# The last quarter of a second MLP product, from four plain tiles to seven quarter products

## The chip, the cores and the metric

One core of a Trainium2 chip runs the whole program in one launch. The metric is the time of an execution in microseconds on the device. The kernel is written by hand in a tile language: the program names tiles and instructions, and a scheduler at compile time orders each engine's instructions (earlier program text first, among those it believes ready), assigns buffers and inserts the waits. Where the text asks for it, an engine's order is fixed as written.

## The reference

Two layers of a hybrid decoder block on 512 tokens of width 1024, all in float32. Each layer has a mixing part (a gated delta rule and a sliding-window attention, both fed by one input projection, merged and projected by `w_o`), and then an MLP:

```python
h2 = rmsnorm(x, pre_mlp_g)
ff = jnp.square(jax.nn.relu(h2 @ w_ff1)) @ w_ff2      # 1024 -> 4096 -> 1024
return x + rmsnorm(ff, post_mlp_g)
```

The change is in `@ w_ff2` and in what follows it: the norm of `ff`, the residual, and the norm with which the next layer begins.

## The kernel before

**Products in three parts.** TensorE multiplies pairs of rounded values. Every float32 operand is split into a high part (a cast on ScalarE) and a low part (the value less its high part, on VectorE), and a product is the sum of high x high, high x low and low x high: three matmuls. `split` (L406, L407) does so for activations, `prefetch` (L319 the cast `wh`, L320 the difference `wl`) for weights.

**Weights in chunks.** All weights are packed in the order in which they are used, as chunks of 128 x 1024 numbers (512 KB; 128 x 864 in the first part of the input projection). `load` (L269) fetches one by a DMA on SyncE's queue (SP) into one of five buffers `wr`; `weights()` hands out the next split chunk and has `prefetch` run four ahead (`LOOK`), each into one of four `wh` and `wl` buffers.

**The MLP in quarters.** `w_ff1` has 4096 columns, taken in four quarters `s` of 1024. In each, `mm_a` forms eight blocks of 128 hidden units x 512 tokens in PSUM (24 matmuls each), ScalarE applies relu and the square, and the quarter's 1024 rows of `w_ff2` are multiplied in. The sum over the quarters is in `acc[t][n]`: four tiles `t` of 128 tokens, two halves `n` of 512 columns.

**Quarters 0 to 2: seven products.** The quarter's product, 512 tokens x 1024 hidden units x 1024 columns, is cut in two in every direction, and a Strassen-Winograd scheme forms it from seven half-size products P1 to P7 in place of eight. `lefts` makes the left factors (sums and differences of halves of the hidden values, then seven splits, on VectorE and ScalarE) for each half of the hidden block. `seven` makes the right factors as a running sum of weight blocks (`add`, L285, on VectorE), in 14 chunks. `mm_c` (L395, L397, L399) does one product: two chunks x two token tiles x two k-blocks x three = 24 matmuls of 512 columns; with `onto` it adds to a PSUM tile that holds an earlier product. The order is P1, P5, P6, P4, P7, P2, P3. Results are drained to `acc` by VectorE or ScalarE (`into`, L1232 and L1234; L1289, L1301, L1309), and six adds of SBUF tiles go to POOL (`ptt`, L1293 and L1303). Tokens 0 and 1 are complete only after P2 and P3, tokens 2 and 3 after P7.

**Quarter 3: plain.** Eight blocks of hidden values are split to `h3`; `mm_b4` multiplies them by the left 512 columns of `w_ff2` for all four tiles, chunk by chunk (L382 to L384), and VectorE adds the result to `acc[t][0]`, ScalarE sums its squares (`meansq`, L426) and VectorE multiplies by the gain (L1328). The right 512 columns follow tile by tile (`mm_b`, L355 to L357), and each finished tile is passed to `ff2_tail`.

**The tail of a tile.** `ff2_tail` calls `post_tile`: load the residual (`xt`, two DMAs, L468, into buffers T[5] and T[6] that quarters 0 to 2 use for the left factors of P1 and P2), add the last product (L471), sum of squares, `rstd` (a sum L433 and a power on POOL, L434), the gain (L474), scale and add the residual (L475, L476). In layer 1 the tile is then written out (L1240). In layer 0 it is stored to `xd` (L1242), `norm_scale` applies the next norm (another two sums of squares, a power on POOL, `xs` on VectorE, L446), and `norm_turn` transposes it (TensorE, L455) and splits it (L459, L461) into the left side of the next layer's projection.

**The order at the boundary.** In layer 0, `last_tiles` does tiles 0 and 1, then tiles 2 and 3 together, with the turns of tiles 0 and 1 put between their k-blocks. The next layer's first projection begins with tiles 0 and 1; the turns of tiles 2 and 3 are put between the halves of tile 1 there. TensorE's order over this whole stretch is fixed as written (`Order`). At the end of layer 1 nothing is fixed: four times `mm_b` and `ff2_tail`.

Of the kernel before, what the change touches and what calls it, by code (L numbers as in the profile page):

```python
# [20 lines left out]
P = 128  # L21
# [31 lines left out]
def chunk_order(depth):  # L53


    out = []
    for l in range(depth):
        a_in = lambda w, c: out.append(("chunk", w, l, 0, c, 0))
        b_in = lambda w, r, c, n: out.append(("chunk", w, l, r, c, n))
        for n in range(3):  # L60
            for j in range(4):
                b_in("w_in", j * 256, OFF_B + n * NB, NB)
        n_ = {"K": 0, "G": 0, "A": 0}
        for c in "".join(MIX):
# [12 lines left out]
        for m in range(KT):  # L77
            a_in("w_up_dn", m * P)
        for n in range(2):
            for j in range(4):  # L80
                b_in("w_o", j * 256, n * 512, 512)
        for s in range(4):
            for m in FF_ORDER if s < 3 else range(8):
                a_in("w_ff1", (s * 8 + m) * P)
            if s < 3:
                out.append(("seven", "w_ff2", l, s * 1024))
                continue
            for n in range(2):
                for j in range(4):
                    b_in("w_ff2", s * 1024 + j * 256, n * 512, 512)  # L90
    return out


# [26 lines left out]
def hybrid_trunk(ctx, tc, x, positions, pre_mix_g, dn_conv_w, dn_a_log, dn_dt_bias, dn_norm_g,  # L120
# [47 lines left out]
    def PM(name):  # L168
        return pm.tile([P, 512], F32, name=name, tag="pm")
# [105 lines left out]
    def seven(w, l, r0):  # L275


        held = {}

        def part(i, k, j):  # L280
            return load((w, l, r0 + i * 512 + j * 256, k * 512, 512))

        def add(j, o):
            a = held["a", j]
            tt(out=a, in0=a, in1=o, op=ALU.add)  # L285
# [13 lines left out]
        return [(lambda f=f, j=j: f(j), 512) for f in makes for j in range(2)]  # L299


    specs = []
    for kind_, *key in chunk_order(depth):
        if kind_ == "seven":
            specs.extend(seven(*key))
        else:
            specs.append((tuple(key), key[4]))
    pre = []
# [15 lines left out]
    def weights():  # L324
        i = used[0]
        used[0] += 1
        prefetch(i + LOOK)
        r, pre[i] = pre[i], None
        return r

    def mm_a(ps, aT, ks=range(KT), w=None):
        wh, wl = w = w or weights()
        for k in ks:
            hi, lo = aT[k]
            mm(ps, lhsT=wh[:, k, :], rhs=hi, start=k == 0, stop=False)  # L335
            mm(ps, lhsT=wh[:, k, :], rhs=lo, start=False, stop=False)  # L336
            mm(ps, lhsT=wl[:, k, :], rhs=hi, start=False, stop=k == KT - 1)  # L337
        return w
# [44 lines left out]
                    mm(pss[t], lhsT=hi[:, tsl], rhs=wl[:, r, :], start=False, stop=False)  # L383
                    mm(pss[t], lhsT=lo[:, tsl], rhs=wh[:, r, :], start=False, stop=k == KT - 1)  # L384

    def mm_c(pss, left, onto=False):

        for j in range(2):
            wh, wl = weights()
            hi, lo = left[j]  # L390
            for t in range(2):
                for r in range(2):
                    c = slice(r * 256 + t * P, r * 256 + (t + 1) * P)
                    first, last = j + r == 0 and not onto, j + r == 2
                    mm(pss[t], lhsT=hi[:, c], rhs=wh[:, r, :], start=first, stop=False,  # L395
                       skip_group_check=onto)
                    mm(pss[t], lhsT=hi[:, c], rhs=wl[:, r, :], start=False, stop=False,  # L397
                       skip_group_check=onto)
                    mm(pss[t], lhsT=lo[:, c], rhs=wh[:, r, :], start=False, stop=last,  # L399
                       skip_group_check=onto)  # L400

    def four(i):
        return [b("ps_b4") for b in ((PZ, PZ, PS, PS) if i % 2 else (PM, PM, PK, PS))]
# [5 lines left out]
    def pair(U, name):  # L409
        return U(name + "_h", F32R), U(name + "_l", F32R)  # L410
# [82 lines left out]
    for l in range(depth):  # L493
# [764 lines left out]
                split(src, *p_)  # L1258
                left[name].append(p_)

        for s in range(3):
            left = {f"P{i}": [] for i in range(1, 8)}
            raw = [None, None]
            for i, m in enumerate(FF_ORDER):
                if s == 0 and i < 4:
                    ps = early[i][0]
                else:
                    ps = PM("ps_f1")
                    mm_a(ps, h2)
# [24 lines left out]
            pc = [PM("ps_p4"), PM("ps_p4")]  # L1294
            mm_c(pc, left["P4"])
            for t in range(2):
                into(2 + t, 0, pc[t])
            pc = [PS("ps_p7"), PK("ps_p7")]
            mm_c(pc, left["P7"])
            for t in range(2):  # L1300
                tt(out=v_[t], in0=pc[t], in1=v_[t], op=ALU.add)  # L1301
                for n, op in ((0, ALU.subtract), (1, ALU.add)):
                    ptt(out=acc[2 + t][n], in0=acc[2 + t][n], in1=v_[t], op=op)  # L1303
            mm_c(pa, left["P2"], True)
            for t in range(2):
                into(t, 0, pa[t])
            mm_c(pb_, left["P3"], True)
            for t in range(2):
                tt(out=acc[t][1], in0=pb_[t], in1=acc[t][1], op=ALU.add)  # L1309


        gb3 = gain(post_mlp_g[l])
        h3 = []
        for m in range(8):
            ps = PM("ps_f1")
            mm_a(ps, h2)
            r_ = T[4]("relu")
            act(out=r_, in_=ps, func=AF.Relu)
            act(out=r_, in_=r_, func=AF.Square)
            p_ = pair(T[m % 4], "h3")  # L1320
            split(r_, *p_)
            h3.append(p_)
        pss = four(1)
        mm_b4(pss, h3)
        for t in range(NT):
            tt(out=acc[t][0], in0=pss[t], in1=acc[t][0], op=ALU.add)
            s0[t] = meansq(acc[t][0], "pq0", True)
            tt(out=acc[t][0], in0=acc[t][0], in1=gb3[:, :512], op=ALU.mult)  # L1328
        ws = [weights() for _ in range(4)]
        if l < depth - 1:  # L1330
            nxt = pre_begin(l + 1)
            xs_next = []
            order = Order(nc.tensor)
            order.begin()
            last_tiles(ws, h3, "ps_f2", ff2_tail, lambda t: norm_turn(xs_next[t], t, nxt[1]))
            hT = nxt
        else:
# [28 lines left out]
```

## Time and profile before

| | us |
|---|---|
| median of 3 runs | 1878.39 (1876.84 to 1881.92) |
| the profiled execution's own time | 1877.79 |
| its span, first to last instruction | 1876.1 |
| TensorE busy | 1847.1 (98%) |
| VectorE busy | 1278.7 (68%) |
| ScalarE busy | 937.7 (50%) |
| POOL busy | 279.9 (15%) |

The span is what the profile shows between the first and the last instruction; the execution's own time has 1.7 us more around it. The profile names the engines PE (TensorE; PEld is its loading of the left operand), DVE (VectorE), ACT (ScalarE), POOL (GpSimd) and SP (SyncE, here the queue of DMAs). L with a number is a line of the kernel; a line of a helper stands for all its callers. A row of a group gives busy time and mean duration, and then the time the engine stood idle before these instructions and what ended it. The granted clock of TensorE was 0.999 of full.

### The profile page before, as it was taken

What the parts mean: (1) busy time and instruction counts of PE and PEld (TensorE: products, weight loads), DVE (VectorE), ACT (ScalarE), POOL (GpSimd) and SP (SyncE); (2) the same over time, 40 slices, a digit from 0 to 9 for tenths busy, and PEclk for the clock granted to TensorE, in tenths of its full rate; (3) what the DMA queues carried; (4) which work ended last, traced back from release to release, by engine and by line L of the source; (5) the groups of instructions that cost most, each with busy time, mean ns of one, the idle gap of its engine ahead of it and who ended that gap; (6) DMA issues with size and microseconds to landing.
All of it is one profiled execution on the core that took longest, in us unless ns stands there. A gap on an engine that the chain in (4) does not pass through costs nothing. (4 is left out here: it accounts for less than half of the span.)

```text
span 1876.1 us, 26833 instructions
## 1 busy us (share of the span) xinstructions
PE 1847.1 (98%) x9716; PEld 1533.0 (82%) x9716; DVE 1278.7 (68%) x2434; ACT 937.7 (50%) x1909; POOL 279.9 (15%) x421
## 2 busy tenths in 40 slices
PE   8999999999999999999999999999999999999998
PEld 7888788888888888888888887888887888888886
DVE  5499795777656667684556997857775567586834
ACT  6677732344434645454456887233343346454442
POOL 1322102121100020211012231022111000111200
PEclk9999999999999999999999999999999999999999
DMA  5633436333363253554245333553334533534631
GB/s 179 201 117 114 122 124 193 103 123 103 90 213 129 87 191 101 169 168 169 84 143 187 103 128 102 161 171 104 122 96 116 190 121 103 178 124 153 196 122 45
DMA packets 123445, 255.40 MB, mean 136 GB/s; under 512 B 32609, under 2 KB 49313, under 8 KB 123314
## 3 DMA queue, kind: packets, MB, share of 16 engines
q1 hardware_dynamic: 123314, 253.71, 42.2%
q8 instruction: 76, 1.25, 0.3%
q14 instruction: 55, 0.45, 0.1%
HBM read 224.70 MB, written 28.97 MB: 135 GB/s over the span
## 5 line engine op out<-in xcount | busy, mean ns | idle before, releaser
L320 DVE TENSOR_TENSOR wl<-wr,wh 128x1024 fp32r<-128x1024 f32 (+1 forms) x332 | 419.0, 1269 | 336.1 <-ACT wh L319 329.2
L319 ACT CAST wh<-wr 128x1024 fp32r<-128x1024 f32 (+1 forms) x332 | 344.2, 1041 | 565.4 <-PE ps_f L336 140.7
L335 PE MATMUL ps_f<-g_h,wh 128*128 128x512 f32 x448 | 174.3, 389 | 0.0
L336 PE MATMUL ps_f<-g_l,wh 128*128 128x512 f32 x448 | 174.3, 389 | 0.0
L337 PE MATMUL ps_f<-g_h,wl 128*128 128x512 f32 x448 | 174.3, 389 | 0.0
L397 PE MATMUL ps_p<-wl,P_h 128*128 128x512 f32 x336 | 131.7, 392 | 2.2 <-DVE wl L320 2.0
L399 PE MATMUL ps_p<-wh,P_l 128*128 128x512 f32 x336 | 130.9, 389 | 0.0
L395 PE MATMUL ps_p<-wh,P_h 128*128 128x512 f32 x336 | 130.8, 389 | 0.0
L335 PEld LDWEIGHTS ps_f<-g_h,wh 128*128 128x128 f32 x448 | 84.1, 188 | 17.5
L337 PEld LDWEIGHTS ps_f<-g_h,wl 128*128 128x128 f32 x448 | 84.1, 188 | 17.4
L336 PEld LDWEIGHTS ps_f<-g_l,wh 128*128 128x128 f32 x448 | 84.1, 188 | 17.4
L397 PEld LDWEIGHTS ps_p<-wl,P_h 128*128 128x128 f32 x336 | 63.1, 188 | 18.5 <-DVE wl L320 5.5
L395 PEld LDWEIGHTS ps_p<-wh,P_h 128*128 128x128 f32 x336 | 63.1, 188 | 13.3
L399 PEld LDWEIGHTS ps_p<-wh,P_l 128*128 128x128 f32 x336 | 63.1, 188 | 12.8
L382 PE MATMUL ps_b<-wh,h_h 128*128 128x432 f32 (+1 forms) x192 | 71.1, 371 | 0.0
L383 PE MATMUL ps_b<-wl,h_h 128*128 128x432 f32 (+1 forms) x192 | 70.4, 367 | 0.0
L384 PE MATMUL ps_b<-wh,h_l 128*128 128x432 f32 (+1 forms) x192 | 70.0, 366 | 0.0
L285 DVE TENSOR_TENSOR wr<-wr 128x1024 f32<-128x1024 f32 x48 | 58.5, 1231 | 1.9 <-DMA wr<-in_weights_dram 1.1
L434 POOL TENSOR_TENSOR pr<-pq,pw 128x1 f32<-128x1 f32 x16 | 9.4, 588 | 329.8 <-DVE pq L433 329.8
L1293 POOL TENSOR_TENSOR acc<-acc,p 128x512 f32<-128x512 f32 x8 | 18.8, 2357 | 258.8 <-DVE p L1289 258.8
L335 PE MATMUL ps_qp<-h_h,wh 128*128 128x512 f32 x128 | 54.9, 429 | 0.0
L336 PE MATMUL ps_qp<-h_l,wh 128*128 128x512 f32 x128 | 54.1, 422 | 0.0
(356 smaller groups left out, 4932.1 us busy)
## 6 DMA issues: line engine op xcount, KB each, us to landing
wr<-in_weights_dram SPq DMA_DIRECT2D x308, 512.0 KB
wr<-in_weights_dram SPq DMA_DIRECT2D x24, 432.0 KB
D<-dd SPq DMA_DIRECT2D x32, 256.0 KB
xd<-xo SPq DMA_DIRECT2D x12, 512.0 KB
xt<-xd SPq DMA_DIRECT2D x24, 256.0 KB
D<-gd SPq DMA_DIRECT2D x16, 256.0 KB
dd<-D SPq DMA_DIRECT2D x16, 256.0 KB
kkd<-kk SPq DMA_DIRECT2D x16, 256.0 KB
```

The costliest lines, as they stand in the source:

```text
L285: tt(out=a, in0=a, in1=o, op=ALU.add)
L319: nc.scalar.copy(wh[:, :w], wr[:, :w])
L320: sub(out=wl[:, :w], in0=wr[:, :w], in1=wh[:, :w].bitcast(F32), op=ALU.subtract)
L335: mm(ps, lhsT=wh[:, k, :], rhs=hi, start=k == 0, stop=False)
L336: mm(ps, lhsT=wh[:, k, :], rhs=lo, start=False, stop=False)
L337: mm(ps, lhsT=wl[:, k, :], rhs=hi, start=False, stop=k == KT - 1)
L382: mm(pss[t], lhsT=hi[:, tsl], rhs=wh[:, r, :], start=k == 0, stop=False)
L383: mm(pss[t], lhsT=hi[:, tsl], rhs=wl[:, r, :], start=False, stop=False)
L384: mm(pss[t], lhsT=lo[:, tsl], rhs=wh[:, r, :], start=False, stop=k == KT - 1)
L395: mm(pss[t], lhsT=hi[:, c], rhs=wh[:, r, :], start=first, stop=False, skip_group_check=onto)
L397: mm(pss[t], lhsT=hi[:, c], rhs=wl[:, r, :], start=False, stop=False, skip_group_check=onto)
L399: mm(pss[t], lhsT=lo[:, c], rhs=wh[:, r, :], start=False, stop=last, skip_group_check=onto)
```

## The change

Quarter 3 is treated like quarters 0 to 2: its product is made of seven, in both layers. Its order is another: P1, P5, P6, then P2 and P3 (which complete tiles 0 and 1), then P4 and P7 (which complete tiles 2 and 3).

- `seven` takes its right factors in that order. The blocks for P2 and P3 are loaded as they are, while the running sum is kept in its two buffers for P4, and the one for P7 is loaded anew: 16 loads of 512 KB for 14 chunks, where the plain quarter had 8.
- After P6, six adds on POOL put `v_` into the second half of tiles 0 and 1 and into both halves of tiles 2 and 3.
- After P2, `first_half` (sum of squares, gain) is done for tiles 0 and 1; after P3, `ff2_tail` for them.
- After P4 comes the drain to the first half of tiles 2 and 3. P7 is subtracted from the first half and, in `ff2_tail`, added to the second half of these tiles.
- In layer 0, the turn of tile 0 stands in the middle of P7 (`mid`), that of tile 1 behind it. At the end of layer 1, P7 is done tile by tile (`by_tile`), with both chunks for one tile before the other.
- `mm_b4`, `mm_b`, `h3` and `last_tiles` are no longer used in quarter 3.

```diff
-            for m in FF_ORDER if s < 3 else range(8):
+            for m in FF_ORDER:
                 a_in("w_ff1", (s * 8 + m) * P)
...
+            out.append(("seven" if s < 3 else "last_seven", "w_ff2", l, s * 1024))
...
+        if last:
+            makes = (*makes[:3], makes[5], lambda j: part(1, 1, j), makes[3],
+                     lambda j: (hold("a", 0, 1, j), add(j, part(1, 1, j)))[1])
...
-    def mm_c(pss, left, onto=False):
+    def mm_c(pss, left, onto=False, mid=None, by_tile=False):
+        ws = [None, None]
+        jt = [(j, t) for j in range(2) for t in range(2)]
+        for j, t in sorted(jt, key=lambda a: a[1]) if by_tile else jt:
+            ws[j] = ws[j] or weights()
...
+            if mid and (j, t) == (0, 1):
+                mid()
...
-        for s in range(3):
+        for s in range(4):
...
+            if s == 3:
+                break
...
-        h3 = []
-        for m in range(8):
-            ps = PM("ps_f1")
-            mm_a(ps, h2)
...
-        pss = four(1)
-        mm_b4(pss, h3)
-        for t in range(NT):
-            tt(out=acc[t][0], in0=pss[t], in1=acc[t][0], op=ALU.add)
+        for t in range(2):
+            for a, op in ((acc[t][1], ALU.add), (acc[2 + t][0], ALU.subtract), (acc[2 + t][1], ALU.add)):
+                ptt(out=a, in0=a, in1=v_[t], op=op)
+
+        def first_half(t):
             s0[t] = meansq(acc[t][0], "pq0", True)
             tt(out=acc[t][0], in0=acc[t][0], in1=gb3[:, :512], op=ALU.mult)
-        ws = [weights() for _ in range(4)]
+
+        mm_c(pa, left["P2"], True)
+        for t in range(2):
+            into(t, 0, pa[t])
+            first_half(t)
         if l < depth - 1:
             nxt = pre_begin(l + 1)
             xs_next = []
             order = Order(nc.tensor)
             order.begin()
-            last_tiles(ws, h3, "ps_f2", ff2_tail, lambda t: norm_turn(xs_next[t], t, nxt[1]))
+        turn = lambda t: norm_turn(xs_next[t], t, nxt[1])
+        mm_c(pb_, left["P3"], True)
+        for t in range(2):
+            ff2_tail(t, pb_[t])
+        pc = [PM("ps_p4"), PM("ps_p4")]
+        mm_c(pc, left["P4"])
+        for t in range(2):
+            into(2 + t, 0, pc[t])
+        pc = [PZ("ps_p7"), PZ("ps_p7")]
+        mm_c(pc, left["P7"], mid=(lambda: turn(0)) if l < depth - 1 else None, by_tile=l == depth - 1)
+        if l < depth - 1:
+            turn(1)
+        for t in range(2):
+            tt(out=acc[2 + t][0], in0=acc[2 + t][0], in1=pc[t], op=ALU.subtract)
+            first_half(2 + t)
+            ff2_tail(2 + t, pc[t])
...
-            for t in range(NT):
-                ps = PM("ps_f2")
-                mm_b(ps, ws, h3, t)
-                ff2_tail(t, ps)
```

More of the change, by code (lines that the diff above doesn't have):

```diff
@@ L273, in blocks, with seven @@
         return a[:, :2 * n_ if n_ else 1024].rearrange("p (k c) -> p k c", k=2 if n_ else 8)
-    def seven(w, l, r0):
+    def seven(w, l, r0, last=False):
         held = {}
@@ L303, in hybrid_trunk @@
     for kind_, *key in chunk_order(depth):
-        if kind_ == "seven":
-            specs.extend(seven(*key))
+        if kind_ != "chunk":
+            specs.extend(seven(*key, last=kind_ == "last_seven"))
         else:
@@ L384, in mm_b4 @@
                     mm(pss[t], lhsT=lo[:, tsl], rhs=wh[:, r, :], start=False, stop=k == KT - 1)
-    def mm_c(pss, left, onto=False):
-        for j in range(2):
-            wh, wl = weights()
-            hi, lo = left[j]
[L391 to L400, printed above, removed]
+    def mm_c(pss, left, onto=False, mid=None, by_tile=False):
[3 more added lines that the diff above has]
+            ws[j] = ws[j] or weights()
+            wh, wl = ws[j]
+            hi, lo = left[j]
+            for r in range(2):
+                c = slice(r * 256 + t * P, r * 256 + (t + 1) * P)
+                first, last = j + r == 0 and not onto, j + r == 2
+                mm(pss[t], lhsT=hi[:, c], rhs=wh[:, r, :], start=first, stop=False,
+                   skip_group_check=onto)
+                mm(pss[t], lhsT=hi[:, c], rhs=wl[:, r, :], start=False, stop=False,
+                   skip_group_check=onto)
+                mm(pss[t], lhsT=lo[:, c], rhs=wh[:, r, :], start=False, stop=last,
+                   skip_group_check=onto)
+            if mid and (j, t) == (0, 1):
+                mid()
     def four(i):
@@ L1334, in hybrid_trunk @@
             order.begin()
-            last_tiles(ws, h3, "ps_f2", ff2_tail, lambda t: norm_turn(xs_next[t], t, nxt[1]))
-            hT = nxt
-        else:
-            for t in range(NT):
-                ps = PM("ps_f2")
-                mm_b(ps, ws, h3, t)
-                ff2_tail(t, ps)
+        turn = lambda t: norm_turn(xs_next[t], t, nxt[1])
[10 more added lines that the diff above has]
+            turn(1)
+        for t in range(2):
+            tt(out=acc[2 + t][0], in0=acc[2 + t][0], in1=pc[t], op=ALU.subtract)
+            first_half(2 + t)
+            ff2_tail(2 + t, pc[t])
+        if l < depth - 1:
+            hT = nxt
 _INS = ['x', 'positions', 'pre_mix_g', 'dn_conv_w', 'dn_a_log', 'dn_dt_bias', 'dn_norm_g',
```

12 lines of the change are left out of this document (removed).

## The prediction

> **What bounds the kernel now.** I read the page's busy shares and slices first, then the busy time by stage, then the instructions at the ends of the stages the change touches.
>
> ```profile
> span 1876.1 us, 26833 instructions
> PE 1847.1 (98%) x9716; PEld 1533.0 (82%) x9716; DVE 1278.7 (68%) x2434; ACT 937.7 (50%) x1909; POOL 279.9 (15%) x421
> DVE  5499795777656667684556997857775567586834
> ```
>
> By these, TensorE bounds the kernel, and VectorE at 68% has room. The share is a mean over unlike stages, though, so I asked for the stages that matter: the seven products of quarter 2 in layer 0 (and the same with the instructions that run past their end), then the last quarter's product with its tails in each layer.
>
> ```profile
> core 0: us, PE busy (x) PEld busy (x) DVE busy (x) ACT busy (x) POOL busy (x), PEclk, DMA share, GB/s
> 813.40:852.80 39.40, 38.63 (x169) 31.37 (x168) 37.19 (x39) 19.72 (x24) 12.50 (x6) 1.00 0.62 206
> 813.40:857.00 43.60, 42.83 (x188) 34.84 (x187) 39.73 (x42) 20.77 (x25) 12.50 (x6) 1.00 0.65 216
> 896.40:955.80 59.40, 56.70 (x266) 47.07 (x264) 36.38 (x64) 24.61 (x51) 5.08 (x8) 1.00 0.31 104
> 1825.50:1873.00 47.50, 43.69 (x193) 35.86 (x191) 23.62 (x38) 12.48 (x24) 2.20 (x4) 1.00 0.09 33
> ```
>
> In a stage of seven products VectorE is busy 37.2 of 39.4 us: it is as full as TensorE. In the plain last quarter it has spare time: 23.0 us in layer 0, 23.9 us in layer 1. The change turns the second kind of stage into the first, and leaves the tails of the layer in it.
>
> **The change part by part.** *Matmuls.* The plain product has 8 k-blocks x 2 column halves x 4 tiles x 3 = 192 matmuls, the seven products 7 x 24 = 168; all are 512 wide. Their pace comes from 192 matmuls in a row:
>
> ```profile
> 852.83 0.39 PE L335 MATMUL ps_f<-g_h,wh 128*128 128x512 f32 x1
> ...
> 896.35 0.39 PE L382 MATMUL ps_b<-wh,h_h 128*128 128x512 f32 x1
> ...
> 955.79 0.30 PE L455 MATMUL ps_n<-ident,xs 128*128 128x128 f32 x1 [1.73 <-DVE xs L446]
> ...
> 1825.51 0.39 PE L382 MATMUL ps_b<-wh,h_h 128*128 128x512 f32 x1
> ```
>
> (896.35 - 852.83)/192 = 0.227 us each (the 0.39 is a length that overlaps the next one). So 24 fewer are worth 5.4 us in each layer, 10.9 us in all, if nothing else binds. The other rows are my landmarks: the last product begins at 896.35 and 1825.51; the transposes of the last token tile (the `norm_turn` of tile 3, inside the next layer's first projection) begin at 955.79, 59.4 us after it, and all of TensorE's work behind them is untouched. In layer 1 the landmark is the last VectorE instruction.
>
> *VectorE.* It decides, so I count its instructions from the first product on. The first table is the product stage of quarter 2, the second the last stage of layer 0.
>
> ```profile
> line engine op names shapes xcount | busy us, mean ns | idle before us <-releasers
> L320 DVE TENSOR_TENSOR wl<-wr,wh 128x1024 fp32r<-128x1024 f32 x15 | 21.2, 1438 | 3.4 <-ACT wh L319 3.4
> L285 DVE TENSOR_TENSOR wr<-wr 128x1024 f32<-128x1024 f32 x5 | 6.0, 1218 | 0.2 <-DMA wr<-in_weights_dram 0.2
> ```
>
> ```profile
> L320 DVE TENSOR_TENSOR wl<-wr,wh 128x1024 fp32r<-128x1024 f32 (+1 forms) x9 | 10.2, 1148 | 15.2 <-ACT wh L319 15.2
> L446 DVE SCALAR_TENSOR_TENSOR xs<-xo,nr,gb 128x512 f32<-128x512 f32 x8 | 5.7, 749 | 2.3 <-POOL nr L434 2.2
> L461 DVE TENSOR_TENSOR h_l<-ps_n,h_h 128x512 fp32r<-128x512 f32 x5 | 3.3, 684 | 0.0
> L475 DVE SCALAR_TENSOR_TENSOR xo<-acc,pr,xt 128x512 f32<-128x512 f32 x4 | 3.0, 752 | 2.6 <-POOL pr L434 2.6
> L476 DVE SCALAR_TENSOR_TENSOR xo<-xo,pr,xt 128x512 f32<-128x512 f32 x4 | 3.0, 746 | 0.0
> L1328 DVE TENSOR_TENSOR acc<-acc,gb 128x512 f32<-128x512 f32 x4 | 2.7, 685 | 0.0
> L474 DVE TENSOR_TENSOR xo<-acc,gb 128x512 f32<-128x512 f32 x4 | 2.7, 689 | 0.1
> ```
>
> Durations overlap the next instruction a little; these starts give the pace:
>
> ```profile
> 814.44 1.22 DVE L320 TENSOR_TENSOR wl<-wr,wh 128x1024 fp32r<-128x1024 f32 x1 [2.35 <-ACT wh L319]
> ...
> 820.47 1.29 DVE L407 TENSOR_TENSOR P_l<-S,P_h 128x512 fp32r<-128x512 f32 x2
> 821.68 1.22 DVE L320 TENSOR_TENSOR wl<-wr,wh 128x1024 fp32r<-128x1024 f32 x1
> 822.81 2.35 DVE L285 TENSOR_TENSOR wr<-wr 128x1024 f32<-128x1024 f32 x2
> ...
> 929.33 1.42 DVE L446 SCALAR_TENSOR_TENSOR xs<-xo,nr,gb 128x512 f32<-128x512 f32 x2 [0.73 <-POOL nr L434]
> 930.66 0.69 DVE L471 TENSOR_TENSOR acc<-ps_f,acc 128x512 f32<-128x512 f32 x1
> ...
> 1872.33 0.75 DVE L476 SCALAR_TENSOR_TENSOR xo<-xo,pr,xt 128x512 f32<-128x512 f32 x1
> ```
>
> A plain 512-wide instruction takes a step of 0.60 us (two in 821.68 - 820.47), a split of a weight chunk 1.13 us, a `scalar_tensor_tensor` 0.67 us (two in 930.66 - 929.33).
>
> Layer 0, new stage: quarter 2's work from its first product on was 39.73 us for 42 instructions, of which 15 splits (11 for its own chunks, 4 already for the stage behind), 5 sums of weights, 10 on the left sides, 12 drains of products. The new stage has the same 42: its looked-ahead chunks, its eight weight sums and its order up to the third product are alike, only the four splits ahead are 864 wide (-0.7 us). To it come the tails, which stay: 8 `xs` and 8 of L475/L476 at 0.67 (10.7), 4 of L1328, 4 of L474, 4 of L461 at 0.60 (7.2; of the five L461 one belongs to a later tile), 16 one-column ones (L433, L428) at an estimated 0.1 (1.6), and two more drains, because product 7 is added to both halves of tiles 2 and 3 (1.2). Sum 39.0 + 20.7 = 59.7 us. All of it stands ahead of the transposes of tile 3, since TensorE's order at the boundary is fixed by hand. Idle time comes on top: about 1.0 us at the start (in quarter 2 the first split began at 814.44, where the stage had begun at 813.40), an estimated 0.6 us inside (the 0.2 of the row of L285 and the 3.4 of L320 less its 2.35 at the start leave up to 1.3), and 1.4 us in the last tile's chain, two waits for POOL's power (0.73, and 2.6/4 by L475's row) with no other work left. Sum 62.7 us against 59.4 us now: **layer 0 +3.3 us**. TensorE's own work to that point is 59.4 less its waits from 896 us on (total, times, longest), less 5.4:
>
> ```profile
> PE ps_n L455 <- DVE xs L446: 2.6, 2, 1.7
> ```
>
> That is 51.4 us, so VectorE and not TensorE sets the end.
>
> Layer 1: no next layer, so no splits ahead (39.73 - 4 x 1.13 = 35.2), no `xs`, no L461: 8 of L475/L476 (5.4), L1328 and L474 (4.8), 8 small ones (0.8), two drains (1.2): 47.4 us, plus 1.0 + 0.6 + 0.7 of idle time: 49.7 us. Now it is 47.6 us from the first product to the last VectorE instruction (1825.51 to 1872.33 + 0.75, 47.57); behind it the same output transfer. **Layer 1 +2.1 us**.
>
> *The port between VectorE and POOL.* Six adds of `acc` go to POOL as in quarter 2, but now all behind product 6. Quarter 2's splits cost 21.2 us where 15 x 1.22 is 18.3, so 2.9 us were lost there, and that is in my 39.73.
>
> ```profile
> 844.27 4.17 DVE L320 TENSOR_TENSOR wl<-wr,wh 128x1024 fp32r<-128x1024 f32 x2
> 843.83 8.09 POOL L1303 TENSOR_TENSOR acc<-acc,p 128x512 f32<-128x512 f32 x4 [5.83 <-DVE p L1301]
> L1303 POOL TENSOR_TENSOR acc<-acc,p x24: 1282/2274/2373, 677.7 to 1778.2; 128x512 f32<-128x512 f32 x24
> ```
>
> Two splits beside POOL's adds took 4.17 us, not 2.35. If none met an add, it is 2.9 us less for each layer; if each add held VectorE for its shortest 1.28 us, 6 x 1.28 = 7.7, 4.8 us more. I take quarter 2's 2.9, the nearest row, since the same number of adds runs beside the same kind of splits. The Trainium skill, "SBUF — State Buffer", section "Who interferes with whom", says that a VectorE instruction with two SBUF inputs and a GpSimd one that reads SBUF exclude each other for a whole instruction; the trace agrees with the 4.17. By the rule's full exclusion, six adds in a row would put the sum 4.8 us higher in each layer.
>
> *Loads.* Sixteen chunks in place of eight (blocks are fetched again for each sum they stand in), 4.2 MB more in each layer. Layer 0 moves 16 x 0.52 + 8 x 0.26 (`xt`) + 4 x 0.44 + 1.0 (`xd`) = 13.3 MB in 62 us, 215 GB/s: quarter 2 moved 216 at a DMA share of 0.65. Hidden, 0 us. If not, the second rival.
>
> *ACT and POOL's powers.* ACT had 20.8 us of 43.6 in quarter 2 and takes the squares of the tails: half full, 0. The first tile's power can stand behind the six adds (13.5 us from product 6, about 31 us into the stage; it is wanted near 30): 0 to 1 us, and VectorE has splits to do meanwhile: 0.
>
> *The first product of the quarter* (`w_ff1`) now ends in 22 left-side instructions, as in quarters 0 to 2, where no wait of TensorE followed: 0, with bounds 0 and the 1.1 us that VectorE stood at the start of the stage.
>
> The sum: 1877.8 (the profiled execution, span 1876.1; 0.6 under the median of the runs, 1878.4) + 3.3 + 2.1 = 1883.2; I say 1883.
>
> **The rivals.** *TensorE stays the bound.* If the splits overtake the tails and the tails find gaps, layer 0 saves 5.4 us and pays 1.4 us for the two steps (subtract, gain) that now stand ahead of each late tile's chain; layer 1 saves 5.4 and pays 1.4 to 2.4, as both last tiles' chains now begin 2.7 us apart on one VectorE (5.4 before). Together -7.5: 1870. For it speak the 98% and that VectorE's work can shift within a stage; against it that the sum of that work is longer than the stage, wherever it shifts.
>
> *The queue of loads stalls (slower).* The second halves of `xt` live in the buffers of product 2's left side, so their loads wait, on SP's queue, until product 2 is done, about 22 us into the stage; behind them stand the chunks of products 4 and 7, each the sum of two loads.
>
> ```profile
> SPq L468 <- PE ps_p L399: 6.5, 2, 4.4
> ```
>
> Quarter 2 had this wait, 4.4 us at the longest, at a point where no sum of weights was still to come. If it falls ahead of product 4's or 7's chunk, VectorE stands with nothing to split: up to 4.4 us in each layer, 8.8: 1892. It decides once the wait is longer than the slack: with two of the five buffers held for the sum, three chunks are ahead at 12 x 0.227 = 2.7 us each, and one takes 2.4 us to load (0.52 MB at quarter 2's 216 GB/s) and 1.1 each to sum and to split, so 8.2 - 4.6 = 3.6 us. Against it: the scheduler can issue these loads behind the chunks.
>
> *The half of the tokens isn't done early.* If tiles 0 and 1 are turned no earlier than now, nothing but the lost matmuls is left; that is the forecast itself with its waits in another place.
>
> **How the numbers follow.** My forecast 0.48, TensorE as bound 0.25, stalled loads 0.27. A measurement of this kernel tells a change from none at about 0.3%, 5.6 us (1872.8 to 1884.0). The forecast's own range, by the port's bounds in one layer at a time and the idle time, is 1877 to 1889: of its 0.48 about 0.35 lie within 0.3% and 0.13 above. So faster 0.25, same 0.35, slower 0.40. The range reaches to 1868 (the first rival with the port at no cost in one layer) and to 1894 (the second with 2 us of port).
>
> **What would show it.** Right: in the new stage VectorE busy over 90% from the first product to the tails; waits of TensorE for `wl` (L320) in products 4 and 7 and for `xs` at the turns of tiles 0 to 3, together 8 us or more in layer 0; the step from first product to tile 3's turn 62 to 63 us; in layer 1 the last VectorE instruction 49 to 50 us after the first product. Wrong: VectorE idle for more than 5 us in that stage while TensorE has no wait (the first rival), or waits of VectorE or ACT for `wr` loads (the second).

## The result, and the profile after

The changed kernel takes 1896.35 us (median, 1894.60 to 1897.18), the kernel before beside it 1879.08 us (1876.84 to 1881.92): a ratio of 1.0090 (95% interval 1.0072 to 1.0107), 17 us slower. The direction was forecast, the size was not: 1883 us was said, and 1894 was the end of the range. Times below are the start times of rows of one profiled execution each; for the changed kernel that execution has a span of 1894.3 us.

The page of the changed kernel says that TensorE is as busy as it was (98%) and VectorE a little busier (71% after 68%):

```profile
span 1894.3 us, 26887 instructions
PE 1848.5 (98%) x9668; PEld 1531.0 (81%) x9668; DVE 1340.4 (71%) x2502; ACT 956.7 (51%) x1937; POOL 305.3 (16%) x433
```

TensorE has 48 matmuls fewer and 1.4 us more of busy time. The matmuls got longer, and the view of busy time by stage says where. First the stage of layer 0 from P1 to tile 3's turn, then that of layer 1 from P1 to the last VectorE instruction, then three short stretches (the granted clock is the number behind POOL's):

```profile
897.60:965.30 67.70, 57.57 (x242) 46.90 (x241) 62.27 (x91) 33.90 (x64) 17.24 (x14) 0.90 0.56 189
1834.40:1891.30 56.90, 42.53 (x169) 32.46 (x167) 49.01 (x64) 21.86 (x37) 14.76 (x10) 0.90 0.43 145
...
939.00:942.00 3.00, 2.27 (x10) 1.77 (x9) 3.00 (x6) 3.00 (x9) 0.00 (x0) 0.50 0.44 178
...
956.00:959.00 3.00, 3.00 (x9) 2.77 (x10) 2.56 (x5) 0.25 (x2) 1.29 (x2) 0.50 0.56 193
...
1877.00:1880.00 3.00, 2.94 (x6) 1.93 (x7) 1.23 (x2) 0.00 (x0) 0.00 (x0) 0.50 0.00 0
```

VectorE is the fuller engine in both stages (62.3 of 67.7 us and 49.0 of 56.9; before, by the rows in the prediction, 36.4 of 59.4 and 23.6 of 47.5), and in both the mean clock of TensorE is 0.90 where it was 1.00. What TensorE waits for, first around layer 0's stage, then layer 1's (total, times, longest):

```profile
PE ps_b L354 <- DVE wl L318: 5.0, 1, 5.0
PE ps_n L457 <- DVE xs L448: 3.0, 1, 3.0
...
PE ps_p L395 <- ACT wh L317: 4.7, 2, 4.6
```

All of it is VectorE's work or, with `wh`, a cast that follows a sum of weights on VectorE (L280). On TensorE's own timeline these waits stand at three places, each with slow matmuls behind it:

```profile
897.57 0.39 PE L395 MATMUL ps_p<-wh,P_h 128*128 128x512 f32 x1
...
938.65 1.97 PE L457 MATMUL ps_n<-ident,xs 128*128 128x128 f32 x8 [2.98 <-DVE xs L448]
...
955.88 0.73 PE L354 MATMUL ps_b<-wl,h_h 128*128 128x432 f32 x1 [4.99 <-DVE wl L318]
956.41 0.56 PE L355 MATMUL ps_b<-wh,h_l 128*128 128x432 f32 x1
956.77 0.56 PE L353 MATMUL ps_b<-wh,h_h 128*128 128x432 f32 x1
...
965.29 1.03 PE L457 MATMUL ps_n<-ident,xs 128*128 128x128 f32 x8
...
975.48 0.25 PE L566 MATMUL ps_cw<-ident,cwr 96*128 96x96 f32 x1
...
1834.36 0.39 PE L395 MATMUL ps_p<-wh,P_h 128*128 128x512 f32 x1
...
1877.03 1.22 PE L395 MATMUL ps_p<-wh,P_h 128*128 128x512 f32 x2 [4.56 <-ACT wh L317]
...
1881.86 0.63 PE L397 MATMUL ps_p<-wl,P_h 128*128 128x512 f32 x1
1882.29 0.63 PE L399 MATMUL ps_p<-wh,P_l 128*128 128x512 f32 x1
```

Two landmarks carry the comparison of all kernels. In layer 0 it is the way from P1 to the first instruction behind the next layer's first projection (`ps_cw`): 975.48 - 897.57 = 77.9 us, and before

```profile
966.24 0.25 PE L564 MATMUL ps_cw<-ident,cwr 96*128 96x96 f32 x1
...
1868.80 0.39 PE L357 MATMUL ps_f<-wh,h_l 128*128 128x512 f32 x1
```

966.24 - 896.35 = 69.9 us: 8.0 us more. In layer 1 it is the way from P1 to the end of the span: 1894.3 - 1834.36 = 59.9 us, before 1876.1 - 1825.51 = 50.6: 9.3 us more. Together 17.3 of the 18.2 us between the two spans; the rest lies within the microsecond or two by which the untouched parts differ from one execution to the next.

The rows of busy time say what became of the 5.4 us of matmuls that were saved in each layer. In layer 0's stage TensorE was busy 56.7 us before; 24 matmuls less would leave 51.3, and it is 57.6: 6.3 us more, in matmuls that take longer. Its waits grew from 2.6 to 9.9 us (with three short ones that the view lists beside the rows above). 6.3 + 7.3 - 5.4 = 8.2 of the 8.3 us by which the stage is longer (67.7 after 59.4). In layer 1's stage it was busy 43.7 us, 38.2 without the 24 matmuls, and is 42.5: 4.3 us more; its waits are 5.9 us where it had none. And behind the start of TensorE's last matmul VectorE needs 9.0 us (1882.29 to 1890.50 + 0.75) where it needed 4.3 (1868.80 to 1872.33 + 0.75). 4.3 + 5.9 + 4.7 - 5.4 = 9.5, and the stage is 9.3 us longer.

VectorE's order at two of the places, on its timeline:

```profile
949.14 0.68 DVE L1348 TENSOR_TENSOR acc<-acc,ps_p 128x512 f32<-128x512 f32 x1
...
954.78 1.04 DVE L318 TENSOR_TENSOR wl<-wr,wh 128x864 fp32r<-128x864 f32 x1
...
1869.54 0.15 DVE L435 TENSOR_TENSOR pq<-pq,pq 128x1 f32<-128x1 f32 x1
...
1874.60 1.22 DVE L280 TENSOR_TENSOR wr<-wr 128x1024 f32<-128x1024 f32 x1
...
1877.00 1.22 DVE L318 TENSOR_TENSOR wl<-wr,wh 128x1024 fp32r<-128x1024 f32 x1
1880.82 0.69 DVE L1348 TENSOR_TENSOR acc<-acc,ps_p 128x512 f32<-128x512 f32 x1 [2.60 <-PE ps_p L399]
...
1890.50 0.75 DVE L478 SCALAR_TENSOR_TENSOR xo<-xo,pr,xt 128x512 f32<-128x512 f32 x1
```

In layer 0 the split of the fourth chunk of the next projection (954.78) stands behind the tail of tile 2, which began at 949.14; TensorE has nothing else and stands for 5.0 us. In layer 1 the tails of tiles 0 and 1 (from 1869.54) go ahead of the sum and the split of P7's second chunk; TensorE stands 4.6 us for it, goes on at half clock, and now VectorE waits for TensorE (2.6 us at 1880.82). There each engine waits for the other in turn, so neither stays packed.

### The profile page after: what moved, and what is told of

It reads as the page before. It is cut to its first block, busy times and chain, and to the rows that moved or that the text cites. A ratio compares the mean times of both kernels' runs of the same rounds, so it can differ in the third digit from the quotient of the medians.

```text
span 1894.3 us, 26887 instructions
## 1 busy us (share of the span) xinstructions
PE 1848.5 (98%) x9668; PEld 1531.0 (81%) x9668; DVE 1340.4 (71%) x2502; ACT 956.7 (51%) x1937; POOL 305.3 (16%) x433
## 5 line engine op out<-in xcount | busy, mean ns | idle before, releaser
L397 PE MATMUL ps_p<-wl,P_h 128*128 128x512 f32 x448 | 178.0, 397 | 4.7 <-DVE wl L318 2.8
L395 PE MATMUL ps_p<-wh,P_h 128*128 128x512 f32 x448 | 176.4, 394 | 4.9 <-ACT wh L317 4.7
L399 PE MATMUL ps_p<-wh,P_l 128*128 128x512 f32 x448 | 176.0, 393 | 0.0
L397 PEld LDWEIGHTS ps_p<-wl,P_h 128*128 128x128 f32 x448 | 85.0, 190 | 28.8 <-DVE wl L318 11.3
L399 PEld LDWEIGHTS ps_p<-wh,P_l 128*128 128x128 f32 x448 | 85.1, 190 | 17.2
L335 PEld LDWEIGHTS ps_f<-g_h,wl 128*128 128x128 f32 x448 | 84.1, 188 | 17.5
L280 DVE TENSOR_TENSOR wr<-wr 128x1024 f32<-128x1024 f32 x64 | 80.9, 1275 | 2.3 <-DMA wr<-in_weights_dram 1.6
L1298 POOL TENSOR_TENSOR acc<-acc,p 128x512 f32<-128x512 f32 x8 | 20.0, 2510 | 256.7 <-DVE p L1291 256.7
L1308 POOL TENSOR_TENSOR acc<-acc,p 128x512 f32<-128x512 f32 x24 | 47.4, 2004 | 38.6 <-DVE p L1306 30.8
L866 ACT ACTIVATE M<-M,nm 128x128 f32<-128x128 f32 x128 | 49.9, 392 | 5.9 <-DVE nm L861 5.9
L335 PE MATMUL ps_qp<-h_h,wl 128*128 128x512 f32 x128 | 52.4, 409 | 0.0
L335 PE MATMUL ps_vp<-h_h,wl 128*128 128x512 f32 x128 | 52.3, 409 | 0.0
```

Source lines behind the costliest of these rows:

```text
L866: act(out=M[:, j * P:(j + 1) * P], in_=M[:, j * P:(j + 1) * P], func=AF.Exp, bias=nm[:, j:j + 1], accum_out=den[:, j:j + 1])
```

## The experiments

The first column of numbers is the ratio to the kernel before, measured beside it, with its 95% interval; the others are the two landmarks, from one profiled execution each.

| kernel | us | ratio | layer 0 | layer 1 |
|---|---|---|---|---|
| before | 1879.08 | 1 | 69.9 | 50.6 |
| changed | 1896.35 | 1.0090 (1.0072 to 1.0107) | 77.9 | 59.9 |
| e1 weights first | 1894.81 | 1.0079 (1.0061 to 1.0098) | 78.4 | 56.1 |
| e2 fill | 1893.52 | 1.0075 (1.0060 to 1.0090) | 76.9 | 59.3 |
| e3 no sums | 1878.82 | 0.9996 (0.9986 to 1.0005) | 71.9 | 50.0 |
| e4 adds on VectorE | 1889.57 | 1.0048 (1.0031 to 1.0065) | 75.8 | 56.5 |
| e5 = e1 + e4 | 1892.08 | 1.0067 (1.0050 to 1.0084) | 80.0 | 54.7 |
| e6 = e1 + e3 + e4 | 1881.06 | 1.0014 (1.0004 to 1.0023) | 72.2 | 48.8 |
| e7 the quarters' order | 1889.35 | 1.0053 (1.0038 to 1.0068) | 76.3 | 55.4 |
| e8 before, more VectorE work | 1881.51 | 1.0011 (1.0001 to 1.0020) | 73.6 | 51.0 |
| e9 halves exchanged | 1886.55 | 1.0042 (1.0028 to 1.0056) | 76.4 | 53.4 |
| e10 = e9, no sums | 1882.58 | 1.0014 (1.0006 to 1.0023) | 73.2 | 50.7 |

**e1: the weights ahead of the tails.** Is the order on VectorE the trouble, or its fullness?

```diff
         mm_c(pb_, left["P3"], True)
+        prefetch(used[0] + LOOK)
...
         mm_c(pc, left["P4"])
+        prefetch(used[0] + LOOK)
...
         mm_c(pc, left["P7"], mid=...)
+        prefetch(used[0] + LOOK)
```

> Only the order of the text differs from the changed kernel: the weights of the second half of P7, and the fourth chunk of the next layer's projection, are asked for ahead of the tails of tiles 0 and 1 (2 and 3) and not behind them. Theory ORDER (VectorE works off tails while TensorE waits for a split that stands behind them): the waits of 4.6 us (layer 1, ahead of P7's second chunk) and 5.0 us (layer 0, in the next layer's projection) go, and the stretches at half clock behind them; 8 to 14 us faster than the changed kernel, 1882 to 1888. Theory FULL (the sum of VectorE's work sets the end, in whatever order): the same work, at most 2 us faster, 1894 to 1896.

TensorE's waits in layer 0, the changed kernel's 5.0 for `wl` being gone:

```profile
PE ps_n L457 <- DVE xs L448: 9.0, 3, 4.0
```

The wait changed its name: what was for weights is now 9.0 us for the turns. Layer 0 gains nothing (78.4), layer 1, where no turn is waited for, 3.8 us. In layer 0 the order only chooses who is late. The median is 1.5 us under the changed kernel's, where the order theory expected 8 to 14; the two intervals overlap, so a gain isn't shown. The profiled execution was the fastest of four (1889.85 us), which may flatter the landmarks.

**e2: unused matmuls where TensorE waited,** 48 in all, to keep the clock up.

```diff
+            for _ in range(n):
+                mm(ps, lhsT=ones_r, rhs=fill, start=True, stop=True)
```

> Adds 48 matmuls whose result nobody uses, in the three places where TensorE stood longest: 12 ahead of the turn of tile 0 (wait 3.0 us), 18 ahead of the last two k-blocks of tile 0 in the next layer's projection (5.0 us), 18 ahead of P7 in layer 1 (4.6 us); VectorE's order stays as it is. Theory CLOCK (a wait of 3 us and more halves TensorE's clock for the matmuls behind it, granted clock 0.50 there): at full clock the 10 + 17 + 15 matmuls take 0.2 us less each, 6 to 9 us faster than the changed kernel where nothing else binds, 1887 to 1890. Theory FULL: TensorE's pace behind its waits doesn't matter, within 1 us, 1895 to 1897.

Busy time by stage, at one of layer 0's places and at layer 1's:

```profile
938.00:945.00 7.00, 4.91 (x25) 3.48 (x24) 6.94 (x12) 5.23 (x10) 0.55 (x2) 1.00 0.68 236
...
1877.00:1880.00 3.00, 2.48 (x6) 1.99 (x7) 0.51 (x2) 0.00 (x0) 0.00 (x0) 0.61 0.00 0
```

In layer 0 the clock stayed at 1.00 and the way to the landmark became 1.0 us shorter; in layer 1 the fill did not cover the wait. The median, 1893.52, lies between the two theories (1887 to 1890 and 1895 to 1897), and the intervals of this kernel and the changed one overlap: the slow clock is there, but its own share can't be told from noise.

**e3: the sums of weights left out in the last quarter.**

```diff
-            tt(out=a, in0=a, in1=o, op=ALU.add)
+            if not last:
+                tt(out=a, in0=a, in1=o, op=ALU.add)
```

> Leaves out the eight sums of weight blocks of the last quarter in each layer (the blocks are loaded, the running sum stays the first block). VectorE has 8 x 1.13 = 9.0 us less work in each layer, 5 of the 8 behind the first product (5.7 us). Theory FULL: the end comes earlier by that work, 10 to 12 us in all, 1884 to 1886. Theory ORDER: the tails still stand ahead of the splits, so the two long waits shrink by one sum each and stay, 2 to 5 us, 1891 to 1894.

Busy time of the two stages, P1 to tile 3's turn and P1 to the last VectorE instruction:

```profile
896.90:958.20 61.30, 54.08 (x242) 45.17 (x241) 54.38 (x84) 34.26 (x64) 17.32 (x14) 0.94 0.57 195
1828.00:1875.00 47.00, 38.27 (x169) 31.36 (x167) 42.10 (x59) 22.17 (x37) 14.16 (x10) 0.96 0.46 157
```

The time falls by 17.5 us (1896.35 to 1878.82), more than either theory expected (1884 to 1886, 1891 to 1894). VectorE's busy time in the stages falls by 7.9 and 6.9 us: five sums of a layer stand behind P1, 5.7 us at a step of 1.13, and beside POOL's adds they took longer, as e4 shows. The stages themselves become shorter by 6.4 and 9.9 us, with the waits and the slow clock. In layer 1 TensorE has no wait left; in layer 0 it still stands 4.5 us for `wl` and 2.6 for `xs`. So the slowdown comes with the sums on VectorE: without them it is gone. But a kernel with 48 matmuls fewer and no sums at all only ties with the kernel before, so something else takes the gain.

**e4: the six adds on VectorE instead of POOL.**

```diff
-                ptt(out=a, in0=a, in1=v_[t], op=op)
+                tt(out=a, in0=a, in1=v_[t], op=op)
```

> The six adds of the last quarter go from POOL to VectorE. VectorE gains 6 x 0.60 = 3.6 us of work in each layer and loses the time it stands against POOL: in the changed kernel's layer 1 seven instructions beside the adds took about 4.6 us longer than elsewhere. Theory FULL: 1 us less in each layer, 1894 to 1895. If the port costs only the 2.9 us that quarter 2 showed: 0.7 us more in each, 1897 to 1898. If the tails of tiles 0 and 1 had waited for POOL's adds, more than 2 us faster in each layer.

This gives VectorE six more instructions (3.7 us) in each layer, and the kernel is 6.8 us faster, 2.1 and 3.4 us on the landmarks. A part of the reason stands on the two timelines of the changed kernel:

```profile
914.80 11.48 POOL L1320 TENSOR_TENSOR acc<-acc,p 128x512 f32<-128x512 f32 x6 [61.53 <-DVE p L1291]
```

```profile
916.48 1.95 DVE L318 TENSOR_TENSOR wl<-wr,wh 128x1024 fp32r<-128x1024 f32 x1 [1.16 <-ACT wh L317]
918.35 2.31 DVE L280 TENSOR_TENSOR wr<-wr 128x1024 f32<-128x1024 f32 x1
920.58 0.68 DVE L1236 TENSOR_TENSOR acc<-ps_p,acc 128x512 f32<-128x512 f32 x1
921.18 1.72 DVE L280 TENSOR_TENSOR wr<-wr 128x1024 f32<-128x1024 f32 x1
922.82 2.31 DVE L318 TENSOR_TENSOR wl<-wr,wh 128x1024 fp32r<-128x1024 f32 x1
...
925.13 1.71 DVE L1324 TENSOR_TENSOR acc<-acc,gb 128x512 f32<-128x512 f32 x1
```

Beside the six adds the five instructions with both inputs in SBUF last 10.0 us, where 4 x 1.22 + 0.68 = 5.6 is their length alone; the one at 920.58, which reads PSUM, keeps its 0.68. That is 4.4 us, 0.7 more than the adds cost VectorE itself. In layer 1 the 11 splits and the 5 sums, first in the changed kernel, then with the adds moved:

```profile
L318 DVE TENSOR_TENSOR wl<-wr,wh 128x1024 fp32r<-128x1024 f32 x11 | 15.2, 1397 | 3.5 <-ACT wh L317 3.4
L280 DVE TENSOR_TENSOR wr<-wr 128x1024 f32<-128x1024 f32 x5 | 7.7, 1534 | 0.0
...
L318 DVE TENSOR_TENSOR wl<-wr,wh 128x1024 fp32r<-128x1024 f32 x11 | 13.1, 1220 | 2.4 <-ACT wh L317 2.4
L280 DVE TENSOR_TENSOR wr<-wr 128x1024 f32<-128x1024 f32 x5 | 6.1, 1218 | 0.5 <-DMA wr<-in_weights_dram 0.5
```

The Trainium skill, "SBUF — State Buffer", section "Who interferes with whom", has such pairs of instructions exclude each other; the trace agrees in kind, and the loss here, 4.4 us for 11.48 us of adds, lies between the 2.9 of quarter 2 and the 7.7 that the prediction worked out for full exclusion.

In all, VectorE's busy time in layer 1 falls only from 49.0 to 47.9 us. That is the 1 us for which the first theory expected 1894 to 1895; the gain is larger, of the size that the third theory gave. Its condition isn't seen, though: in layer 0 of the changed kernel POOL's adds end at 926.28 (914.80 + 11.48), and the tails first use those tiles in L473, at 930.29, without a wait. What differs besides is the order that the scheduler gave VectorE. In layer 1 the sum for P7's second chunk now goes ahead of the tail of tile 1:

```profile
1866.74 1.21 DVE L280 TENSOR_TENSOR wr<-wr 128x1024 f32<-128x1024 f32 x1
```

It starts 36.0 us behind P1 (1830.70), in the changed kernel 40.2 (1874.60 - 1834.36), and TensorE's waits there are 4.3 us in place of 5.9. How the gain divides between the adds and this order stays open.

**e5: e1 and e4 together.**

> The changed kernel with both edits: the weights of P7 and of the next projection asked for ahead of the tails, and the six adds on VectorE. By the stages of the single edits (layer 0: +0.5 and -2.1 us, layer 1: -3.8 and -3.4 us against 77.9 and 59.9), if they add up: layer 0 76.3 us from the first product to the end of the first projection, layer 1 52.7 us to the end, 1887 us. Theory FULL (VectorE's work sets the end once its order is right): layer 0 stays over 74, layer 1 over 51, slower than the kernel before by 6 us or more. Theory ORDER: the two waits were all that was lost, 1880 or less.

They don't add up. Layer 1 comes down to 54.7, but in layer 0 the turns are waited for still longer (10.5 us in four waits), and it is 80.0: splits set ahead of tails delay the turns, whoever does the adds.

**e6: e1, e3 and e4 together,** the sums left out.

> As the run with both edits, and without the eight sums of weight blocks in each layer's last quarter (left out: the sums; the loads stay). VectorE has 9 us less to do in each layer. Theory FULL: with VectorE no longer the bound the shorter product shows at last: layer 0 67 to 71 us (69.9 in the kernel before), layer 1 46 to 49 us (50.6), 1872 to 1877, faster than the kernel before by 3 to 7 us of the 10.9 saved. If something else ate the gain (loads, the tails' own chains): no faster than the run without sums alone, 1878 to 1880.

Layer 1 now has no wait of TensorE in P1 to P7, and takes 48.8 us; layer 0 takes 72.2, no better than e3. The time, 1881.06, lies above what either theory expected. A relieved VectorE does not bring the kernel below the one before: there is a second bound.

**e7: the order of quarters 0 to 2** (P1, P5, P6, P4, P7, P2, P3), 14 loads, the four tails behind all products.

```diff
-            out.append(("seven" if s < 3 else "last_seven", "w_ff2", l, s * 1024))
+            out.append(("seven", "w_ff2", l, s * 1024))
...
-            if s == 3:
-                break
...
+        for t in TAILS:
+            s0[t] = meansq(acc[t][0], "pq0", True)
+            tt(out=acc[t][0], in0=acc[t][0], in1=gb3[:, :512], op=ALU.mult)
+            ff2_tail(t, acc[t][1])
```

> The seven products in the last quarter too, but in the order of the other quarters (P1, P5, P6, P4, P7, P2, P3), 14 loads, the four tails behind all of them and the turns of tiles 0 and 1 behind the tails. VectorE's work is two drains less, TensorE's the same; only the overlap is taken away. Theory FULL: VectorE is busy throughout in either order, so the end moves little: layer 0 76 to 82 us, layer 1 58 to 62 us, 1893 to 1902. If doing half of the tokens first hides the tails behind TensorE's products, taking it away costs two tails of about 5 us in each layer, with TensorE's clock down behind the wait: 1908 to 1920.

Nothing is finished early here, TensorE waits 12.1 us in layer 0 for the turns, and it is still faster than the changed kernel (1.0053 against 1.0090), which neither theory expected (1893 to 1902, 1908 to 1920). VectorE has a little less to do, though: from P1 to the landmarks it is busy 63.5 and 46.0 us, in the changed kernel 66.0 and 49.0.

```profile
PE ps_n L458 <- DVE xs L449: 12.1, 2, 7.8
```

**e8: the kernel before with 24 unused additions on VectorE** (14.4 us at 0.60) in each plain product.

```diff
+        for _ in range(24):
+            tt(out=junk[:, :512], in0=h3[7][0].bitcast(F32), in1=gb3[:, :512], op=ALU.add)
```

> The kernel before, with 24 additions of 512 columns on VectorE that nobody uses, from the first matmul of the plain last product on, 24 x 0.60 = 14.4 us in each layer. Theory FULL: the plain stage had 23 us of VectorE's time to spare, so nothing moves: within 2 us of the kernel before in each layer. If VectorE's work costs time wherever it stands: up to 29 us slower.

2 us for 29 us of added work. The room that the prediction read off the stage's busy time was there: nearly all of it in layer 1 (0.4 us longer), less in layer 0 (3.7, more than the 2 expected), where a split stood behind the added work and TensorE waited 2.6 us for it.

**e9: half of the tokens first without the new order.** The row halves of the hidden block are exchanged, so that P1, P5, P6, P4, P7 complete tiles 0 and 1, and P2 and P3, which need no sums, complete tiles 2 and 3. Two adds stay on POOL; four go to VectorE.

```diff
             a11, a21, a12, a22 = X[:, 0:512], ...
+            if s == 3:
+                a11, a21, a12, a22 = a21, a11, a22, a12
...
+        mm_c(pc, left["P7"])
+        for t in range(2):
...
+            ff2_tail(t, acc[t][1])
+        mm_c(pa, left["P2"], True)
...
+        mm_c(pb_, left["P3"], True, mid=..., by_tile=l == depth - 1)
```

> Half of the tokens still first, but by the order of quarters 0 to 2: the two row halves of the hidden block are exchanged in the last quarter, so that P1, P5, P6, P4, P7 complete tiles 0 and 1, and P2 and P3, whose weights need no sum, complete tiles 2 and 3. 14 loads, all five sums of weights ahead of the first tail, two adds on POOL and four on VectorE, the turns of tiles 0 and 1 inside and behind P3. If what costs is where the tails stand (ahead of weights that TensorE still waits for, with six adds of POOL beside them), the long waits for wl and xs go: layer 0 from P1 to the next layer's second product 72 to 74 us (changed kernel 77.9, before 69.9), layer 1 from P1 to the end 50 to 52 us (59.9 and 50.6), 1879 to 1885 us. If only the amount of work on VectorE counts, it is no better than the quarters' order with all tails behind it: 76 and 55 us, 1887 to 1891 us.

TensorE's waits in layer 0, and those in layer 1:

```profile
PE ps_n L454 <- DVE xs L445: 4.3, 3, 3.3
PE ps_n L454 <- DVE h_l L460: 2.5, 2, 1.9
PE ps_b L351 <- DVE nq L427: 2.4, 1, 2.4
...
PE ps_p L394 <- DVE wl L315: 1.7, 2, 1.0
```

It lies between what the two theories expected (1879 to 1885 and 1887 to 1891). The long waits for weights have shrunk, as the order theory had it: in layer 1 from 4.6 to 1.0 us, in layer 0 from 5.0 to 2.4 (the third row; the split of that chunk stands just ahead of the `nq` it names). Layer 1 gains 6.5 us; but 1.5 us is all that layer 0 gains, as the turns are late instead and the waits add up to 10.1 us (9.9 in the changed kernel). Of all versions of the change that leave nothing out it has the lowest median, 9.8 us under the changed kernel, and still 1.0042 of the kernel before; its interval overlaps those of e4 and e7. It changes the order and the place of four adds at once, so by itself it doesn't say which of them helped.

**e10: e9 with the sums left out.**

> The exchanged order with the weight sums of the last quarter left out (their products then use unsummed weights). If VectorE's work alone is the bound, these 5.6 us less behind P1 and the ones ahead of it show in each layer, and with 24 matmuls fewer the kernel gets below the kernel before: layer 0 66 to 68 us, layer 1 45 to 47 us, 1866 to 1872 us. If the tails behind the last product are a second bound, as they were with sums left out and splits first (72.2 and 48.8 us), it stays at 70 to 72 and 48 to 50 us: 1876 to 1881 us.

It is the second bound again (73.2 and 50.7; the time is even 1.6 us above the range given for it). Layer 1 shows it without anything else in the way: TensorE does all seven products with one wait of 0.3 us, and ends 1869.00 - 1830.38 = 38.6 us after P1 began, 4.7 us earlier than before (1868.80 - 1825.51 = 43.3). TensorE's first and last matmul there, and VectorE behind the last:

```profile
1830.38 0.39 PE L393 MATMUL ps_p<-wh,P_h 128*128 128x512 f32 x1
...
1869.00 0.39 PE L397 MATMUL ps_p<-wh,P_l 128*128 128x512 f32 x1
```

```profile
1869.74 0.68 DVE L471 TENSOR_TENSOR acc<-ps_p,acc 128x512 f32<-128x512 f32 x1
...
1877.27 0.75 DVE L476 SCALAR_TENSOR_TENSOR xo<-xo,pr,xt 128x512 f32<-128x512 f32 x1
```

From the last matmul's start to the last VectorE instruction's end are 9.0 us. In the kernel before it was 4.3 (1868.80 to 1872.33 + 0.75): one tile's second half. Here the last products finish two tiles at once, with drains and gains of both still to do. 4.7 us saved on TensorE, 4.7 us paid behind it. e3 has the same in the changed kernel's own order, without a wait of TensorE in layer 1:

```profile
1865.88 0.39 PE L400 MATMUL ps_p<-wh,P_l 128*128 128x512 f32 x1
```

```profile
1874.24 0.75 DVE L479 SCALAR_TENSOR_TENSOR xo<-xo,pr,xt 128x512 f32<-128x512 f32 x1
```

From P1 (1828.03) that is 37.9 us to the last matmul, 5.4 less than before, the whole of the 24 matmuls; and 9.1 us behind it, 4.8 more.

## Why the prediction was right in direction and wrong in size

*Right.* VectorE is the engine whose work costs the time: TensorE's waits are for it, and without the sums the slowdown is gone (e3). The plain stage had the room (e8). The loads cost little: e3 keeps all sixteen and the slowdown is gone, no sum of weights in either stage of the changed kernel waited for a load, and one cast of layer 1, at 1852.1, waited 2.4 us for its chunk, of which VectorE stood 1.0. So the rival of the stalled queue, up to 4.4 us in each layer, is not what happened. The rival of TensorE as the bound, with a gain, is out too, and e3 and e10 say why even without the sums there is no gain: the prediction put the longer end of layer 1 at 1.4 to 2.4 us, and it is 4.7.

*Wrong: the idle time of VectorE, the step "plus 1.0 + 0.6 + 0.7 of idle time" and its twin in layer 0.* In layer 1 VectorE's work was forecast at 47.4 us and is 49.0; its idle time was forecast at 2.3 and is 7.9 (56.9 - 49.0). This term alone is 5.6 of the 7.2 us missing there. On the timeline 3.5 us of it are two waits for products that TensorE had not finished (2.60 and 0.85), for which the sum had no term; 2.1 are waits for POOL's powers, one for each tile, where 0.7 stood for the last; 2.1 are for casts, 1.0 of them at the start, as forecast. I took it that a VectorE with more work than TensorE stays packed whatever the order of its work. In layer 1 it doesn't: tails that stand ahead of a chunk that TensorE needs make TensorE stop, and then VectorE waits for the late product. In layer 0 the work to tile 3's `xs` is 60.8 us (62.27 less 1.45 of a later split and a copy) against 59.7, and the idle time 5.6 against 3.0: 2.5 us in five waits for POOL's powers (1.4 stood for two), 2.2 for casts and 0.5 for a sum of squares on ScalarE, none for a product. Then TensorE, held up in its slowed projection, comes 1.3 us late to the turn. These are the 5.0 us by which 67.7 exceeds 62.7.

How much of this is the order's doing is shown only in part. e1 changes nothing but the order, and only its layer 1 is shorter. e7 and e9 are 7 and 10 us faster than the changed kernel, but VectorE has less work in them too (from P1 to the landmarks 2.5 and 3.0 us less in e7, 1.9 and 2.4 in e9), and moving the adds alone brought 6.8 us (e4).

*Wrong: the port, 2.9 us per layer.* Six adds in a row cost 4.4 us in layer 0, within the bounds given (0 to 7.7), 1.5 us over the value taken. Quarter 2's adds came in two groups, with drains from PSUM among the splits; here they stand where VectorE does splits and sums.

*Left out: the clock.* The sum had no term for matmuls at half speed behind a wait; with them TensorE was busy 6.3 and 4.3 us longer in the two stages than the count of its matmuls asks for. The prediction's range had no case in which two of these terms went wrong in both layers at once, which is what happened.

*What it said would show.* VectorE over 90% to the tails: 29.1 of the first 31.3 us in layer 1, 93%, yes. Waits of 8 us or more in layer 0: 9.9 in all, but at the places named, products 4 and 7 and the turns, only 4.9; the 5.0 for `wl` stand in the next layer's projection, which it did not name. And they were not spread: two long ones, and behind these the clock went down. Tile 3's turn at 62 to 63 us: no, 67.7; layer 1's last VectorE instruction at 49 to 50: no, 56.9. Half of the tokens done early: turn 0 was 35.4 us behind P1 before (931.71) and is 41.1 now; of all versions of the change none got under 36.3 (e6).

*What stays open.* How much the half clock costs by itself: at full clock (e2, layer 0) TensorE mostly waited instead, and 1.0 us was left. How the order and the adds share what e4, e7 and e9 gain. And why layer 0 keeps 3.3 us in e10 with neither sums nor waits for weights in the products: its turns still wait (4.1 us for `xs`, 3.4 for `h_l`) and the next projection 2.3 for `wl`, but no run took the tails' length away.

## What to carry to other kernels

Read the busy shares in the stage that changes, and count the second engine's work there instruction by instruction: an engine at 68% of the whole can be full in one stage. When two engines are both near full, a ledger of busy times is a lower bound only; the order in which the second engine serves the first has to be written down, each item with who waits for it. And count what is left behind the last product: fewer matmuls in an order that finishes two tiles at once moved the time from TensorE to the tail, 4.7 us for 4.7 (e10, layer 1).

## What the runs showed of the hardware

In the changed kernel the granted clock is 0.50 behind each of three waits of TensorE, of 2.98, 4.99 and 4.56 us, for about 6 us (from 938.65, 955.88 and 1877.03 on): a 512-wide matmul then takes a step of 0.43 us (1881.86 to 1882.29) instead of 0.23, a 432-wide one 0.36 (956.41 to 956.77) instead of 0.20. In the kernel before, behind a wait of 1.7 us, it stayed at 1.00. The length of the single wait doesn't decide it alone: the clock is 0.50 behind a wait of 2.62 us in e3 (935.04), there for 3.4 us, and behind one of 1.84 us in e4 (936.14), for 6.8 us from 937.05 on; in e6 it stays at 1.00 for more than 5 us behind one of 2.38 us (950.57). The Trainium skill, "TensorE: Matmul & The Clock Gate", section "HAM oscillation — how this bites in real kernels", says that waiting gaps over about 3.4 us bring the half clock back; the trace agrees with 4.56 and 4.99, and shows it behind the shorter waits above too, 2.98, 2.62 and 1.84 us. I had not priced it, because the prediction spread TensorE's waits over many short ones.

Moving six additions from POOL to VectorE, the fuller engine, made the kernel 7 us faster (e4); VectorE's order changed with it.
